# A two-layer decoder in which both feed-forward blocks go from fp32r pairs to pairs of 16-bit floats under powers of two found on the chip, and the token factor goes into the tokens

## The chip, the cores and the metric

The kernel runs on one core of one Trainium2 chip. The metric is the device time in microseconds of one execution, and lower is better. A core has five engines that run their own instruction queues in order: TensorE (PE: matmuls and their weight loads), VectorE (DVE), ScalarE (ACT), GpSimd (POOL) and SyncE (SP, which here starts all the DMA transfers). They wait for each other by semaphores. SBUF is the working memory and PSUM holds the results of matmuls.

## The reference, cut to what matters

1024 tokens of 1024 features run through two layers. Layer 0 mixes three branches of sparse attention and one with sinks, layer 1 a mixture of dilated window attentions; both are followed by a feed-forward block, and this block is what the change is about.

```
D_MODEL = 1024; SEQ = 1024; DEPTH = 2; FFN_HIDDEN = 2816
def rms_norm(x, g):
    y = x * lax.rsqrt(jnp.mean(x * x, axis=-1, keepdims=True) + NORM_EPS)
    return y * g

for layer in range(DEPTH):
    h = rms_norm(x, attn_norm[layer])
    x = x + mixer(h) @ w_out                     # attention of this layer
    h = rms_norm(x, ffn_norm[layer])
    gate, up = jnp.split(h @ w_gate_up[layer], 2, axis=-1)
    x = x + (jax.nn.silu(gate) * up) @ w_down[layer]
return rms_norm(x, final_norm)
```

All inputs are float32.

## The kernel before, in words

**Products of pairs.** Each float32 operand is split in two fp32r tiles: the high part is a rounded copy (ACT), the low part is what is left (`tensor_sub` on DVE or POOL). `gemm` then makes three matmuls for each 128 rows of the contraction: high weight by high token, high by low, low by high. A matmul has a 128x128 weight and 512 columns of tokens, that is, one of two halves of the sequence (`h` is 0 or 1), and adds into a bank of PSUM (`pD`, three of them).

**Feed-forward.** `ffn_jobs` runs over 22 blocks of 128 hidden features (`fi`), gathered in chunks: blocks 0 and 1, then five chunks of four. For each block there is a gate job and an up job (24 matmuls each), for each chunk `down_jobs` with as many weight tiles as the chunk has blocks. The last chunk of the very last block is done by `last_job`. The tokens `n.hT` are only scaled by the gains; the factor 1/rms of each token (`n.R`, made in `norm_close` by a matmul that spreads it over all partitions) is put in after the matmul, in `gated`: gate times R on DVE, tanh on ACT, a product on DVE, a product with R/2. `upped` multiplies by the up result and splits the hidden tile in a pair. `evac` adds the down result to the residual.

**Weights.** Every weight tile is 128x1024 floats (512 KB). `loads` starts its DMA, `splits` makes the high copy on ACT, `lows` the low part on DVE or POOL, whichever `vg` thinks is free sooner. They run some weights ahead of the job that needs them (`loads=4`, `splits=3` in ORDER). A weight takes three tiles of the S4 arena while it is split and two until its job is done. Each weight is loaded and split twice, once for either half of the sequence.

**Order.** The program is written by a list scheduler in Python (`run`): small tasks yield the engine they need next, and the task that could start soonest by a table of costs (`COST`, `LAT`, `SELF`) is written next. The cost of a matmul is the same for 16-bit and fp32r tiles of 512 columns there. The jobs (`dense`) are in this order: projections of layer 0; then for h = 0 and h = 1 the output projection, the feed-forward block and the projections of layer 1; then for h = 0 and h = 1 the output projection and feed-forward block of layer 1. Attention is woven in between: that of layer 0, h = 1 runs beside the first feed-forward block (layer 0, h = 0), that of layer 1, h = 1 beside the third (layer 1, h = 0), part of layer 1, h = 0 beside the second, nothing beside the last. All instructions are recorded by one helper, so that they all have line 209 in the profile; groups are told apart by tiles: `pD` holds projections, `pT` and `pS` scores and small things, `pO` attention outputs; `S` are the large and half-size SBUF tiles, `SM` tiny ones of 128x8.

Of the kernel before, what the change touches and what calls it, by code (L numbers as in the profile page):

```python
# [10 lines left out]
F32 = mybir.dt.float32  # L11
# [16 lines left out]
NF = FFN // P  # L28
SCALE = 0.125
# [4 lines left out]
MAGIC = float(0x5F3759DF)  # L34
INF = float("inf")
# [108 lines left out]
class W:  # L144


    def __init__(self, load, views=None):
        self.load, self.views = load, views
        self.st = self.h = self.l = None
        self.ok = False  # L150

    def split(self, k):
        c = slice(k * P, (k + 1) * P)
        return self.h.w[:, c], self.l.w[:, c]
# [5 lines left out]
    def drop(self):  # L160
        self.h.drop()
        self.l.drop()

# [19 lines left out]
class Norm:  # L183
    def __init__(self):
        self.hT, self.acc, self.ss, self.n = {}, None, None, 0
        self.r = self.R = self.R2 = self.CR = self.SR = self.CK = self.SK = None
        self.uses, self.pairs = 0, False

# [37 lines left out]
class Kernel:  # L226
# [80 lines left out]
    def est(self, *bufs):  # L307

        t = 0.0
        for b in bufs:  # L310
            i = self.info.get((b.raw if isinstance(b, Buf) else b).tensor.name)
            if i is not None:
                t = max(t, i[0])
        return t
# [98 lines left out]
    def more_constants(self):  # L413
        nc, io = self.nc, self.io
        self.sinks = self.const.tile([P, 8], F32, name="sinks", tag="sinks")
        self.sinks8 = self.const.tile([P, 8], F32, name="sinks8", tag="sinks8")
        yield "s"
        self.dma(self.sinks, io["sinks"][0:1, :].to_broadcast([P, 8]))
        for g, src in zip(self.gains[1:], (io["attn_norm"][1], io["ffn_norm"][0], io["ffn_norm"][1], io["final_norm"])):
            yield "s"  # L420
            self.dma(g, src.rearrange("(k p) -> p k", p=P))
        yield "v"
        nc.vector.tensor_scalar(self.sinks8, self.sinks, 1.0 / SCALE, None, op0=ALU.mult)

# [85 lines left out]
    def splits(self):  # L510
        for i, w in enumerate(self.wreq):
            self.wsp = i

            def cond():
                if w.st is None:
                    return INF
                here = self.ends[self.jobi]
                if i < here:
                    return max(self.est(w.st), self.S4.when(2))
                if i >= max(here + self.o.splits, self.ends[self.jobi + 1]):  # L520
                    return INF
                return max(self.est(w.st), self.S4.when(2, RES))
            yield "a", cond
            w.h, w.l = self.S4.take(), self.S4.take()
            for h, l, s in w.parts():
                self.nc.scalar.copy(h, s)
# [22 lines left out]
    def wready(self, w):  # L549
        return self.est(w.h, w.l) if w.ok else INF  # L550
# [27 lines left out]
    def wcols(self, wt, c0):  # L578

        return W(lambda st: self.dma(st.rearrange("p (k c) -> p k c", c=P),  # L580
                                     wt[:, c0:c0 + P].rearrange("(k p) c -> p k c", p=P)))
# [47 lines left out]
    def norm_close(self, n, kind, half=None):  # L629
# [56 lines left out]
        if kind == "ffn":  # L686
            yield "a", self.S2.when
            n.R2 = self.S2.take()
            nc.scalar.activation(n.R2.t, R.t, AF.Copy, scale=0.5)
            y.drop()  # L690
        n.R = R
        for i, b in enumerate(tabs):
            yield "v"
            nc.vector.tensor_mul(b.t, b.t, R.t)
            setattr(n, tables[i][1], b)

# [399 lines left out]
    def cmp_prep(self, key, pe):  # L1096

        nc = self.nc
        pet = self.const.tile([32, 2, 64], F32, tag="pe" + key, name="pe" + key)
        yield "s"  # L1100
        for hh in range(2):
            self.dma(pet[:, hh, :], pe)
        yield "p", lambda: max(self.pS.when(), self.est(pet)) if self.jobi > 1 else INF
# [5 lines left out]
        ps.drop()  # L1109
        yield "vg", lambda: 0.0 if self.zn.get(key, [0, 0])[1] == 2 else INF  # L1110
# [901 lines left out]
    def gu_jobs(self, wt, fi, n, hid, at):  # L2012
# [3 lines left out]
        def gated(acc):  # L2016
# [12 lines left out]
            state["s"] = s  # L2029

        def upped(acc):
            yield "v", self.of(lambda: state.get("s"))
            s = state["s"]
            nc.vector.tensor_mul(s.t, acc.t, s.t)
            acc.drop()
            yield "a", self.S4.when
            t = self.S4.take()
            nc.scalar.copy(t.x[:, 0], s.t)
            yield "vg"
            self.vg(HT, self.o.slack / 2).tensor_sub(t.x[:, 1], s.t, f(t.x[:, 0]))  # L2040
            s.drop()
            hid[at] = t

        def gate(w):
            acc = yield from self.new_acc()
            yield from self.gemm(acc.t, self.stat(w), n.hT.get, KT)
            self.go(gated(acc), 2)

        def up(w):
            acc = yield from self.new_acc()  # L2050
            yield from self.gemm(acc.t, self.stat(w), n.hT.get, KT)
            if fi == NF - 1:
                for b in n.hT.values():
                    b.drop()
            self.go(upped(acc), 2)
        n.uses += 1
        return [Job(24 * MM, gate, [self.wcols(wt, fi * P)]), Job(24 * MM, up, [self.wcols(wt, FFN + fi * P)])]

    def down_jobs(self, wt, fs, hid, h, turn, final):
# [5 lines left out]
        def evac(d, acc):  # L2065
            x = self.xs[h][d]
            yield "v", lambda: 0.0 if x[1] == turn else INF
            self.nc.vector.tensor_add(x[0].t, acc.t, x[0].t)
            acc.drop()
            x[1] += 1  # L2070
            if final:
                yield from final(d, x[0])

        for c in range(nk):
# [4 lines left out]
            def run(w, c=c):  # L2079
                for dd in range(cw // P):  # L2080
                    d = c * (cw // P) + dd

                    def stat(k, tile=False):
                        o = slice(k * cw + dd * P, k * cw + (dd + 1) * P)
                        return w if tile else (w.h.w[:, o], w.l.w[:, o])
                    acc = yield from self.new_acc()
                    yield from self.gemm(acc.t, stat, hid.get, nk)
                    self.go(evac(d, acc), 2)
                if c == nk - 1:
                    for b in hid.values():  # L2090
                        b.drop()
            jobs.append(Job(24 * MM, run, [W(load)]))
# [124 lines left out]
    def ffn_jobs(self, layer, h, n, final):  # L2217
        wg, wd = self.io["w_gate_up"][layer], self.io["w_down"][layer]
        jobs = []
        chunks = [[0, 1]] + [list(range(c, c + 4)) for c in range(2, NF, 4)]  # L2220
        pend = None
        for ci, fs in enumerate(chunks):
            hid = {}
            for i, fi in enumerate(fs):
                jobs += self.gu_jobs(wg, fi, n, hid, i)
# [4 lines left out]
            else:  # L2230
                pend = self.down_jobs(wd, fs, hid, h, ci, final if fs is chunks[-1] else None)
# [69 lines left out]
    def whole(self):  # L2301
# [15 lines left out]
        self.gains = [self.const.tile([P, KT], F32, name=f"gains{i}", tag=f"gains{i}") for i in range(5)]  # L2317
        self.constants()
# [170 lines left out]
```

## Time and profile before

| | |
|---|---|
| time, median of 3 runs | 2752.99 us (2748.75 to 2753.67) |
| the profiled execution | 2751.49 us, of it 2749.7 from the first to the last instruction (the span) |
| mean granted TensorE clock | 0.979 of full speed |
| DMA traffic | 373.85 MB, mean 136 GB/s |

Busy time of an engine is given as a share of the span or of a stretch. Matmuls overlap in the profile, since their ends are modelled: the time of one in a dense row is read from the distance of starts or from the count in a stretch, not from its mean duration.

### The profile page before, as it was taken

To read this page: it belongs to the slowest core of one execution; us is meant where nothing else is said; L and a number is where in the kernel's file an instruction comes from. 1 tells how busy PE (TensorE), PEld (TensorE's weight loads), DVE (VectorE), ACT (ScalarE), POOL (GpSimd) and SP (SyncE) were. 2 spreads that over 40 slices of the span, in tenths; PEclk is the share of its full clock that TensorE was granted. 3 is DMA by queue.
4 is the path that set the end of the run, shared out by engine and by line. 5 is a ranking of instruction groups with operands and counts; after the bars stand their busy time and mean duration, and the time that the engine had idled before them with its cause. 6 is when DMAs were issued, how large, how long until landed. Compare 5 with 4: busy or idle time off the path is not lost. (4 is left out here: it accounts for less than half of the span.)

```text
span 2749.7 us, 40587 instructions
## 1 busy us (share of the span) xinstructions
PE 2635.3 (96%) x15186; PEld 2167.0 (79%) x15186; DVE 1681.4 (61%) x3328; ACT 1146.3 (42%) x1913; POOL 1179.0 (43%) x723
## 2 busy tenths in 40 slices
PE   8888889999999999999999999899999999999998
PEld 7767777777877888778788888778888888788887
DVE  6898877666666785555445667656566665433334
ACT  6465555444444554333333454333333345322222
POOL 4454544433433566444443546343313225544442
PEclk9999999999999999999999999899999999999999
DMA  8765585222332335834344456844544444433330
GB/s 233 211 165 163 155 240 149 74 81 74 105 104 81 119 125 191 250 104 125 94 120 119 140 167 188 234 124 119 155 125 136 130 133 143 140 96 92 100 99 31
DMA packets 447368, 373.85 MB, mean 136 GB/s; under 512 B 54342, under 2 KB 383942, under 8 KB 447172
## 3 DMA queue, kind: packets, MB, share of 16 engines
q1 hardware_dynamic: 447172, 371.26, 46.8%
q8 instruction: 120, 1.97, 0.3%
q14 instruction: 76, 0.62, 0.1%
HBM read 301.42 MB, written 65.30 MB: 133 GB/s over the span
## 5 line engine op out<-in xcount | busy, mean ns | idle before, releaser
L209 PE MATMUL pD<-S,S 128*128 128x512 f32 (+2 forms) x9648 | 2266.5, 388 | 20.5 <-DVE S L209 12.7
L209 PEld LDWEIGHTS pD<-S,S 128*128 128x128 f32 x9648 | 1738.0, 191 | 378.3 <-DVE S L209 15.9
L209 POOL TENSOR_TENSOR S<-S,S 128x1024 fp32r<-128x1024 f32 (+2 forms) x535 | 1023.0, 1925 | 1147.4 <-ACT S L209 618.1
L209 DVE TENSOR_TENSOR S<-pD,S 128x512 f32<-128x512 f32 (+1 forms) x526 | 355.2, 680 | 533.0 <-PE pD L209 514.1
L209 ACT CAST S<-S 128x1024 fp32r<-128x1024 f32 (+2 forms) x571 | 540.2, 984 | 309.3 <-DVE S L209 202.6
L209 DVE TENSOR_TENSOR S<-S,S 128x1024 fp32r<-128x1024 f32 (+4 forms) x243 | 360.9, 1490 | 89.9 <-ACT S L209 88.0
L209 ACT ACTIVATE S<-pT 128x512 f32<-128x512 f32 (+3 forms) x304 | 171.3, 567 | 505.7 <-DVE pT L209 444.4
L209 DVE TENSOR_TENSOR PH<-S,PH 128x512 f16<-128x512 f32 (+3 forms) x265 | 231.4, 877 | 70.8 <-ACT PH L209 69.7
L209 PE MATMUL pT<-S,S 128*128 128x128 f32 (+11 forms) x1072 | 223.7, 336 | 4.1 <-DMA S<-NM 2.5
L209 ACT ACTIVATE S<-S 128x512 f32<-128x512 f32 (+1 forms) x172 | 103.1, 600 | 278.2 <-DVE S L209 277.2
L209 PEld LDWEIGHTS pT<-S,S 128*128 128x128 f32 (+2 forms) x1072 | 196.0, 224 | 24.1 <-DMA S<-NM 3.2
L209 ACT CAST PH<-S 128x512 f16<-128x512 f32 (+3 forms) x304 | 177.1, 589 | 8.5 <-PE pO L209 2.1
L209 PEld LDWEIGHTS <-PH 128*128 128x128 f16 (+1 forms) x3384 | 117.4, 99 | 54.6 <-issue 36.0
L209 DVE TENSOR_TENSOR pT<-pT,S 128x512 f32<-128x512 f32 (+4 forms) x176 | 91.5, 524 | 87.0 <-PE pT L209 86.4
L209 PE MATMUL pO<-S,PH 128*128 128x65 f16 (+1 forms) x3192 | 131.9, 196 | 10.5 <-DVE PH L209 7.2
L209 PE MATMUL pS<-S,S 128*128 128x512 f32 (+3 forms) x460 | 117.9, 348 | 20.1 <-DVE SM L209 13.5
L209 POOL TENSOR_TENSOR PH<-S,PH 128x512 f16<-128x512 f32 (+2 forms) x39 | 48.7, 1250 | 144.4 <-ACT PH L209 144.2
L209 PEld LDWEIGHTS pS<-S,S 128*128 128x128 f32 (+1 forms) x460 | 82.4, 213 | 35.2 <-DVE SM L209 18.7
L209 DVE TENSOR_TENSOR pT<-pT,tDE 128x128 f32<-128x128 f32 (+2 forms) x176 | 64.7, 373 | 70.2 <-PE pT L209 69.3
L209 DVE CUSTOM_DVE_ANT_0 junk<-pS,S 128x256 bf16<-128x256 f32 (+1 forms) x192 | 85.2, 444 | 23.4 <-PE pS L209 16.6
L209 DVE CUSTOM_DVE_ANT_0 junk<-pS,mW 128x512 bf16<-128x512 f32 (+3 forms) x160 | 84.0, 525 | 14.2 <-PE pS L209 8.7
L209 DVE SCALAR_TENSOR_TENSOR S<-S,S 128x512 f32<-128x512 f32 x88 | 67.5, 767 | 38.8 <-ACT S L209 37.8
(163 smaller groups left out, 1028.7 us busy)
## 6 DMA issues: line engine op xcount, KB each, us to landing
S<-in_w_gate_up SPq DMA_DIRECT2D x176, 512.0 KB
S<-in_w_down SPq DMA_DIRECT2D x88, 512.0 KB
S<-in_w_qkv_o SPq DMA_DIRECT2D x48, 512.0 KB
S<-in_w_in_e SPq DMA_DIRECT2D x22, 512.0 KB
mixd<-S SPq DMA_DIRECT2D x18, 512.0 KB
S<-mixd SPq DMA_DIRECT2D x18, 512.0 KB
xd<-S SPq DMA_DIRECT2D x32, 256.0 KB
S<-dhq SPq DMA_DIRECT2D x64, 128.0 KB
```

What stands on the lines that cost most here:

```text
L209: return fn(*a, **kw)
```

## The change

Blocks 2 to 21 of gate and up (`fi >= WIDE`) and the down products of the four middle chunks (`DOWN16`) multiply pairs of float16 instead of fp32r pairs. High and low part of a weight stand side by side in one tile (`W16`). A weight tile is scaled by a power of two: when a tile is loaded for the first time (h = 0), ACT sums its squares (`splits`), a one-column matmul with a tile of ones sums them over the partitions (`over`), four DVE instructions make the power of two and its inverse from the bits of that sum (`power`), and only then is the high part made (`high`) and the low part, on DVE alone (`lows`). For h = 1 the power is known already (`self.scales`). The hidden features of a chunk get a power of their own in `chunk16`. The tokens of these blocks are made again by `halves`: times the token factor R, then times the gain and its power of two, as a float16 pair `n.x16`; `gated16`, `upped` and `evac` undo the powers. Blocks 0 and 1 and the last chunk's down product stay as they were. The `pe` tables of `cmp_prep` move to an S2 tile, and `more_constants` prepares the scaled gains.

```diff
+WIDE = 2
+DOWN16 = True
+NW16 = 2 * (NF - WIDE) + 16
...
+class W16(W):
+    def cut(self, c):
+        a = self.h.f16(2048)
+        return a[:, c], a[:, 1024 + c.start:1024 + c.stop]
...
+            w.h = self.S4.take()
+            if isinstance(w, W16):
+                if w.scale:
+                    self.high(w)
+                else:
+                    acc = self.SM.take()
+                    self.nc.scalar.activation(w.cut(slice(0, 1024))[0], f(w.st.w), AF.Square, accum_out=acc.t[:, 0:1])
+                    self.go(self.ranged(w, acc), lambda i=i: 1 if i < self.ends[self.jobi] + 1 else 3)
+            else:
+                w.l = self.S4.take()
+                for h, l, s in w.parts():
+                    self.nc.scalar.copy(h, s)
+                w.split_ = True
...
+    def high(self, w):
+        self.nc.scalar.activation(w.cut(slice(0, 1024))[0], f(w.st.w), AF.Copy, scale=w.scale["s"])
+        w.split_ = True
+    def power(self, total, out, inv, top=RAISE):
+        nc, i = self.nc, I32
+        nc.vector.tensor_scalar(inv, total, 1e-30, None, op0=ALU.max)
+        nc.vector.tensor_scalar(out.bitcast(i), inv.bitcast(i), -0.5, top, op0=ALU.mult, op1=ALU.add)
+        nc.vector.tensor_scalar(out.bitcast(i), out.bitcast(i), FIELD, None, op0=ALU.bitwise_and)
+        nc.vector.tensor_scalar(inv.bitcast(i), out.bitcast(i), -1.0, float(0x7F000000), op0=ALU.mult, op1=ALU.add)
+    def over(self, acc, n):
+        yield "p", self.pS.when
+        ps = self.pS.take()
+        self.nc.tensor.matmul(ps.t[:, 0:n], self.ones, acc.t[:, 0:n], start=True, stop=True)
+        acc.drop()
+        yield "v"
+        return ps
+    def ranged(self, w, acc):
+        ps = yield from self.over(acc, 1)
+        k = self.wscn % (2 * NW16)
+        self.wscn += 2
+        out, inv = self.wsc[:, k:k + 1], self.wsc[:, k + 1:k + 2]
+        self.power(ps.t[:, 0:1], out, inv)
+        ps.drop()
+        w.scale.update(s=out, inv=inv)
+        yield "a"
+        self.high(w)
...
     def lows(self):
         for i, w in enumerate(self.wreq):
-            yield "vg", lambda: INF if self.wsp <= i else self.est(w.h)
+            yield "v" if isinstance(w, W16) else "vg", lambda: self.est(w.h) if w.split_ else INF
             urgent = i < self.ends[self.jobi] + 1
+            if isinstance(w, W16):
+                h, l = w.cut(slice(0, 1024))
+                self.nc.vector.scalar_tensor_tensor(l, f(w.st.w), w.scale["s"], h, op0=ALU.mult, op1=ALU.subtract)
+                w.st.drop()
+                w.ok = True
+                continue
...
+            for d in range(KT):
+                self.go(self.halves(n, d), 3)
...
+    def halves(self, n, d):
+        nc = self.nc
+        x, g = self.xs[n.half][d][0], n.g16[:, d:d + 1]
+        yield "vg", self.S2.when
+        t = self.S2.take()
+        self.vg(HT).tensor_mul(t.t, x.t, n.R.t)
+        self.used(n)
...
+        b = n.x16s[d // 2]
+        x = b.f16(2048).rearrange("p (d s c) -> p d s c", d=2, s=2)[:, d % 2]
+        nc.scalar.activation(x[:, 0], t.t, AF.Copy, scale=g)
+        yield "v"
+        nc.vector.scalar_tensor_tensor(x[:, 1], t.t, g, x[:, 0], op0=ALU.mult, op1=ALU.subtract)
+        t.drop()
+        n.x16[d] = View(b, x)
...
+        def gated16(acc, w):
+            yield "v", self.SM.when
+            cb = self.SM.take()
+            nc.vector.scalar_tensor_tensor(cb.t[:, 0:1], w.scale["inv"], 0.5, n.g16[:, KT + 1:KT + 2], op0=ALU.mult,
+                                           op1=ALU.mult)
...
+            nc.scalar.activation(s, acc.t, AF.Tanh, scale=cb.t[:, 0:1])
+            yield "v"
+            nc.vector.scalar_tensor_tensor(s, s, 1.0, acc.t, op0=ALU.add, op1=ALU.mult)
             acc.drop()
+            state["c"], state["s"], state["b"] = cb, s, b
...
+            if half:
+                c = state["c"].t
+                nc.vector.scalar_tensor_tensor(c[:, 1:2], w.scale["inv"], n.g16[:, KT + 1:KT + 2], c[:, 0:1], op0=ALU.mult,
+                                               op1=ALU.mult)
+                nc.vector.scalar_tensor_tensor(s, acc.t, c[:, 1:2], s, op0=ALU.mult, op1=ALU.mult)
+                state["c"].drop()
+            else:
+                nc.vector.tensor_mul(s, acc.t, s)
...
+    def chunk16(self, room, hid, at, s):
+        nc = self.nc
...
+        x = [t.f16(2048).rearrange("p (d s c) -> p d s c", d=2, s=2)[:, d] for t in room["tiles"] for d in range(2)]
+        nc.scalar.activation(x[at][:, 0], s, AF.Square, accum_out=room["acc"].t[:, at:at + 1])
+        room["s"][at] = s
+        if len(room["s"]) < 4:
+            return
+        acc, sb = room["acc"], self.SM.take()
+        ps = yield from self.over(acc, 4)
+        sc, inv = sb.t[:, 0:1], sb.t[:, 1:2]
+        nc.vector.tensor_reduce(out=sb.t[:, 2:3], in_=ps.t[:, 0:4], axis=AX.X, op=ALU.add)
+        ps.drop()
+        self.power(sb.t[:, 2:3], sc, inv)
+        room["scale"] = sb
+        def pair(i):
+            yield "a"
+            nc.scalar.activation(x[i][:, 0], room["s"][i], AF.Copy, scale=sc)
+            yield "v"
+            nc.vector.scalar_tensor_tensor(x[i][:, 1], room["s"][i], sc, x[i][:, 0], op0=ALU.mult, op1=ALU.subtract)
...
+            hid[i] = View(room["tiles"][i // 2], x[i])
+        for i in range(4):
+            self.go(pair(i), 2)
...
+            if room is None:
+                self.nc.vector.tensor_add(x[0].t, acc.t, x[0].t)
+            else:
+                sb = room["scale"]
+                self.nc.vector.tensor_mul(sb.t[:, 3 + d % 2:4 + d % 2], sb.t[:, 1:2], w.scale["inv"])
+                self.nc.vector.scalar_tensor_tensor(x[0].t, acc.t, sb.t[:, 3 + d % 2:4 + d % 2], x[0].t, op0=ALU.mult,
+                                                    op1=ALU.add)
...
+            room = {"raw": {}, "read": 0} if 0 < ci < len(chunks) - 1 and DOWN16 else None
```

What stands where in the programs, at three places (names are tile, number and instance; x2 means twice in a row).

PE in the last block, six matmuls of a gate or up job before. Moving tile first, then the weight: the high weight (S_1599) twice, the low one (S_1600) once, and no instruction of its own for loading the weight:

```order
L209 MATMUL pD_25788<-S_1512_24715,S_1599_25677 128x512 x2
L209 MATMUL pD_25788<-S_1512_24715,S_1600_25678 128x512
L209 MATMUL pD_25788<-S_1516_24753,S_1599_25677 128x512 x2
L209 MATMUL pD_25788<-S_1516_24753,S_1600_25678 128x512
```

The same kind of place of the change (last block, a gate or up job):

```order
L242 LDWEIGHTS S_1432_26897
L242 MATMUL pD_27025<-S_1406_26486,S_1432_26897 128x512
L242 LDWEIGHTS S_1432_26897
L242 MATMUL pD_27025<-S_1406_26486,S_1432_26897 128x512
L242 LDWEIGHTS S_1432_26897
L242 MATMUL pD_27025<-S_1406_26486,S_1432_26897 128x512
L242 LDWEIGHTS S_1436_26937
L242 MATMUL pD_27045<-S_1364_25948,S_1436_26937 128x512
```

Each 16-bit matmul has a weight load of its own in the program, and high and low parts are cuts of one tile (S_1432).

PE in the first block (layer 0, h = 0), down products of the first chunk, before:

```order
L209 MATMUL pD_6502<-S_355_6151,S_362_6254 128x512 x2
L209 MATMUL pD_6502<-S_355_6151,S_363_6255 128x512
L209 MATMUL pD_6502<-S_364_6273,S_362_6254 128x512 x2
L209 MATMUL pD_6502<-S_364_6273,S_363_6255 128x512
L209 MATMUL pD_6513<-S_355_6151,S_362_6254 128x512 x2
L209 MATMUL pD_6513<-S_355_6151,S_363_6255 128x512
```

and of the change:

```order
L242 MATMUL pD_6584<-S_356_6221,S_363_6293 128x512 x2
L242 MATMUL pD_6584<-S_356_6221,S_364_6294 128x512
L242 MATMUL pS_6590<-SM_6582,ones 128x1
L242 MATMUL pD_6584<-S_367_6395,S_363_6293 128x512 x2
L242 MATMUL pD_6584<-S_367_6395,S_364_6294 128x512
L242 MATMUL pD_6596<-S_356_6221,S_363_6293 128x512 x2
L242 MATMUL pD_6596<-S_356_6221,S_364_6294 128x512
```

These down products stay in fp32r; a sum over the partitions (`pS_6590`, one column against the ones) has come between two of them.

DVE beside these down products, where their results are added to the residual, before:

```order
L209 TENSOR_TENSOR S_128_5242<-pD_6485,S_128_5242 128x512
L209 TENSOR_TENSOR PH_6491<-S_172_6489,PH_6490 128x512
L209 TENSOR_TENSOR S_131_5324<-pD_6502,S_131_5324 128x512
L209 TENSOR_TENSOR pT_6518<-pT_6518,tDE 128x2x128
L209 TENSOR_TENSOR S_135_5422<-pD_6513,S_135_5422 128x512
L209 TENSOR_TENSOR S_139_5538<-pD_6531,S_139_5538 128x512
L209 TENSOR_TENSOR PH_6537<-S_173_6535,PH_6536 128x512
```

and of the change:

```order
L242 TENSOR_TENSOR S_129_5216<-pD_6567,S_129_5216 128x512
L242 TENSOR_TENSOR PH_6573<-S_180_6571,PH_6572 128x512
L242 TENSOR_SCALAR wsc<-pS_6590 128x1
L242 TENSOR_SCALAR wsc<-wsc 128x1 x3
L242 TENSOR_TENSOR S_133_5336<-pD_6584,S_133_5336 128x512
L242 TENSOR_TENSOR pT_6604<-pT_6604,tDE 128x2x128
L242 TENSOR_TENSOR S_137_5438<-pD_6596,S_137_5438 128x512
L242 SCALAR_TENSOR_TENSOR S_375_6581<-S_370_6478,wsc,S_375_6581 128x1024
L242 TENSOR_TENSOR PH_6626<-S_181_6624,PH_6625 128x512
L242 TENSOR_TENSOR S_140_5530<-pD_6619,S_140_5530 128x512
```

Between the additions stand now the four instructions of a power of two (`wsc`) and a weight's low part of 1024 columns (`S_375`); no low part stood in these rows before.

## Rows read from the trace of the kernel before

**Rows 1.** The page's first part: busy time of each engine, its share of the span, instructions.

```profile
PE 2635.3 (96%) x15186; PEld 2167.0 (79%) x15186; DVE 1681.4 (61%) x3328; ACT 1146.3 (42%) x1913; POOL 1179.0 (43%) x723
```

**Rows 2.** Busy time by stretch of the span: start and end in us, length, busy us (and records) of PE, its weight loads, DVE, ACT and POOL, then the granted clock, the DMA share and GB/s.

```profile
core 0: us, PE busy (x) PEld busy (x) DVE busy (x) ACT busy (x) POOL busy (x), PEclk, DMA share, GB/s
100.00:400.00 300.00, 256.13 (x1869) 207.44 (x1868) 258.02 (x643) 167.55 (x326) 138.37 (x104) 0.91 0.67 194
...
400.00:500.00 100.00, 94.89 (x622) 77.79 (x621) 80.51 (x178) 52.54 (x95) 46.51 (x29) 0.98 0.40 114
500.00:900.00 400.00, 392.85 (x2523) 314.95 (x2522) 249.92 (x489) 171.67 (x280) 148.27 (x88) 1.00 0.32 89
900.00:1000.00 100.00, 97.83 (x674) 81.24 (x673) 80.34 (x158) 56.82 (x93) 55.89 (x33) 1.00 0.40 128
1900.00:2300.00 400.00, 396.19 (x2301) 334.21 (x2302) 250.07 (x553) 150.15 (x258) 118.89 (x85) 1.00 0.50 137
...
2500.00:2600.00 100.00, 100.00 (x432) 80.89 (x431) 34.08 (x36) 27.57 (x33) 50.13 (x28) 1.00 0.32 95
```

**Rows 3.** The chain that ended last, in order of time: start and length in us, engine, tile, count.

```profile
2375.40 334.78 PE pD L209 x1443
```

**Rows 4.** Groups of PE's instructions with the shapes kept apart: count, then busy us and mean ns of one, then idle time before them.

```profile
L209 PE MATMUL pD<-S,S 128*128 128x512 f32 x8400 | 2087.0, 401 | 10.4 <-DVE S L209 7.4 <-DMA S<-mixd 2.9
```

**Rows 5.** PE's instructions in order of time, beside attention: start, length in us, what, count. Two dense groups of 16-bit matmuls (`pO`) and what follows each.

```profile
500.86 0.91 PE L209 MATMUL pO<-S,PH 128*128 128x65 f16 x24
501.60 0.71 PE L209 MATMUL pT<-S,S 128*128 128x512 f32 x2
...
545.81 0.91 PE L209 MATMUL pO<-S,PH 128*128 128x65 f16 x24
546.55 0.42 PE L209 MATMUL pT<-S,kc 128*64 128x512 f32 x1
```

**Rows 6.** The same view around two plain-fp32 matmuls (`pS<-SM,ones`; x2 is one instruction).

```profile
1605.26 3.01 PE L209 MATMUL pD<-S,S 128*128 128x512 f32 x12
1608.20 0.38 PE L209 MATMUL pS<-SM,ones 1*128 1x2 f32 x2
1608.51 0.73 PE L209 MATMUL pD<-S,S 128*128 128x512 f32 x2
...
1731.44 2.26 PE L209 MATMUL pD<-S,S 128*128 128x512 f32 x9
1733.63 0.38 PE L209 MATMUL pS<-SM,ones 1*128 1x2 f32 x2
1733.94 0.97 PE L209 MATMUL pD<-S,S 128*128 128x512 f32 x3
1734.74 0.27 PE L209 MATMUL pS<-ident,MR 128*4 128x128 f32 x1
```

**Rows 7.** Groups of DVE, POOL and ACT instructions with the shapes kept apart (busy us, mean ns of one).

```profile
L209 DVE TENSOR_TENSOR S<-pD,S 128x512 f32<-128x512 f32 x510 | 348.4, 688 | 521.2 <-PE pD L209 502.4 <-DMA S<-xd 7.5 <-ACT S L209 4.0
L209 DVE TENSOR_TENSOR S<-S,S 128x1024 fp32r<-128x1024 f32 x129 | 210.7, 1639 | 30.0 <-ACT S L209 28.5 <-PE pD L209 0.9 <-issue 0.2
...
L209 DVE TENSOR_TENSOR S<-S,S 128x512 fp32r<-128x512 f32 x76 | 106.3, 1401 | 55.5 <-ACT S L209 55.4
L209 DVE SCALAR_TENSOR_TENSOR S<-S,S 128x512 f32<-128x512 f32 x88 | 67.5, 767 | 38.8 <-ACT S L209 37.8
...
L209 DVE SCALAR_TENSOR_TENSOR S<-S,vsc,S 128x512 f16<-128x512 f32 x33 | 35.1, 1068 | 5.6 <-ACT S L209 5.5
...
L209 POOL TENSOR_TENSOR S<-S,S 128x1024 fp32r<-128x1024 f32 x229 | 569.5, 2495 | 369.1 <-ACT S L209 290.8 <-issue 42.1 <-PE pD L209 14.7
...
L209 ACT CAST S<-S 128x1024 fp32r<-128x1024 f32 x358 | 368.0, 1044 | 96.0 <-POOL S L209 43.6 <-DMA S<-in_w_out_o 13.3 <-DMA S<-in_w_qkv_o 10.7
```

**Rows 8.** DVE's instructions on the tiles `SM` and `S`: count, then minimum, median and maximum ns; the last row is the group of the second in the table of groups, with its mean.

```profile
L209 DVE TENSOR_TENSOR SM<-SM x49: 151/162/2383, 28.8 to 2742.3; 128x4 f32<-128x4 f32 x43, 128x2 f32<-128x2 f32 x6
...
L209 DVE TENSOR_SCALAR SM<-SM x27: 141/168/2032, 28.2 to 2740.9; 128x4 int32<-128x4 int32 x9, 1x1 f32<-1x1 f32 x9, 128x4 f32<-128x4 f32 x2, 3x1 f32<-3x1 f32 x2
...
L209 DVE TENSOR_TENSOR S<-S,S x243: 652/1224/3443, 8.2 to 2702.4; 128x1024 fp32r<-128x1024 f32 x65, 128x512 fp32r<-128x512 f32 x38, 128x512 f32<-128x512 f32 x13, 128x816 fp32r<-128x816 f32 x4
...
L209 DVE TENSOR_SCALAR SM<-SM 128x4 int32<-128x4 int32 (+6 forms) x27 | 9.2, 341 | 0.9
```

**Rows 9.** All engines in order of time where the last block begins.

```profile
2362.07 0.69 DVE L209 TENSOR_TENSOR S<-pD,S 128x512 f32<-128x512 f32 x1 [3.32 <-PE pD L209]
2362.79 0.72 ACT L209 ACTIVATE S<-S,gains 128x512 fp32r<-128x512 f32 x1 [3.37 <-DVE S L209]
...
2363.55 0.75 DVE L209 SCALAR_TENSOR_TENSOR S<-S,gains,S 128x512 fp32r<-128x512 f32 x1 [0.79 <-ACT S L209]
...
2375.49 0.59 ACT L209 COPY S<-pS 128x512 f32<-128x512 f32 x1 [7.47 <-PE pS L209]
```

**Rows 10.** PE in order of time: the matmuls that spread the token factor (`pS<-S,ones`) of the first block (layer 0, h = 0) and of the norm after it, the same of the third block (layer 1, h = 0), and the sums for the norm after that.

```profile
464.62 1.07 PE L209 MATMUL pS<-S,ones 128*128 128x512 f32 x2
...
962.58 1.02 PE L209 MATMUL pS<-S,ones 128*128 128x512 f32 x2
...
1838.53 1.02 PE L209 MATMUL pS<-S,ones 128*128 128x512 f32 x2
...
2317.65 0.95 PE L209 MATMUL pS<-onesr,S 128*128 128x2 f32 x8
```

More of the change, by code (lines that the diff above doesn't have):

```diff
@@ L162, in drop, with __init__, cut @@
         self.l.drop()
+class W16(W):
+    def __init__(self, load, scale):
+        super().__init__(load)
+        self.scale = scale
+    def cut(self, c):
+        a = self.h.f16(2048)
+        return a[:, c], a[:, 1024 + c.start:1024 + c.stop]
+    def drop(self):
+        self.h.drop()
+class View:
+    def __init__(self, buf, x):
+        self.raw, self.x = buf.raw, x
 class Heads:
@@ L423, in more_constants @@
         nc.vector.tensor_scalar(self.sinks8, self.sinks, 1.0 / SCALE, None, op0=ALU.mult)
+        for i in (2, 3):
+            yield "a", self.SM.when
+            acc, g = self.SM.take(), self.gains16[i - 2]
+            nc.scalar.activation(g[:, 0:KT], self.gains[i], AF.Square, accum_out=acc.t[:, 0:1])
+            ps = yield from self.over(acc, 1)
+            self.power(ps.t[:, 0:1], g[:, KT:KT + 1], g[:, KT + 1:KT + 2], RAISE - float(5 << 23))
+            ps.drop()
+            nc.vector.tensor_scalar(g[:, 0:KT], self.gains[i], g[:, KT:KT + 1], None, op0=ALU.mult)
     def mask(self, m, conds):
@@ L2009, in out_jobs, with gu_jobs @@
         return jobs
-    def gu_jobs(self, wt, fi, n, hid, at):
+    def gu_jobs(self, wt, layer, fi, n, hid, at, half, room=None):
         nc = self.nc
@@ new lines, in upped @@
+        def upped(acc, w):
+            yield "v", self.of(lambda: state.get("b"))
+            s, b = state["s"], state["b"]
+            if half:
[4 more added lines that the diff above has]
+                state["c"].drop()
+            else:
+                nc.vector.tensor_mul(s, acc.t, s)
+            acc.drop()
+            if room is not None:
+                yield from self.chunk16(room, hid, at, s)
+                return
@@ L2054, in up @@
+            if fi == (NF - 1 if half else WIDE - 1):
+                for b in (n.x16s if half else n.hT).values():
                     b.drop()
[L2055 to L2059, printed above, removed]
+            self.go(upped(acc, w), 2)
+        n.uses += not half
+        sc = [self.scales.setdefault((layer, z, fi), {}) if half else None for z in range(2)]
@@ L2084, in stat @@
                         o = slice(k * cw + dd * P, k * cw + (dd + 1) * P)
-                        return w if tile else (w.h.w[:, o], w.l.w[:, o])
+                        return w if tile else w.cut(o)
                     acc = yield from self.new_acc()
                     yield from self.gemm(acc.t, stat, hid.get, nk)
-                    self.go(evac(d, acc), 2)
+                    self.go(evac(d, acc, w), 2)
                 if c == nk - 1:
-                    for b in hid.values():
+                    for b in hid.values() if room is None else room["tiles"]:
                         b.drop()
-            jobs.append(Job(24 * MM, run, [W(load)]))
+            wq = W(load) if room is None else W16(load, self.scales.setdefault((layer, 2, fs[0], c), {}))
+            jobs.append(Job(24 * MM, run, [wq]))
         return jobs
@@ L2219, in ffn_jobs @@
         jobs = []
+        n.half, n.g16 = h, self.gains16[layer]
+        n.uses += KT
         chunks = [[0, 1]] + [list(range(c, c + 4)) for c in range(2, NF, 4)]
@@ L2230, in ffn_jobs @@
             else:
-                pend = self.down_jobs(wd, fs, hid, h, ci, final if fs is chunks[-1] else None)
+                pend = self.down_jobs(wd, layer, fs, hid, h, ci, final if fs is chunks[-1] else None, n, room)
         return jobs + pend
```

103 lines of the change are left out of this document (69 added, 34 removed).

## The prediction, made blind

> **What bounds the kernel now.** I began with the page's busy times: TensorE (PE) is busy in 96% of the span, VectorE (DVE) in 61%, ScalarE (ACT) in 42%, GpSimd (POOL) in 43% [rows 1]. The table by stretch shows where PE is not full: from 100 to 400 us it is at 85% with DVE at 86%, while in the feed-forward blocks (500 to 900 and 1900 to 2300 hold most of the first half's block of layer 0 and of layer 1, 2500 to 2600 lies inside the last block) it is at 98 to 100% at a granted clock of 1.00, that is 2.4 GHz [rows 2]. The chain that ended last agrees: its longest piece is 1443 projection matmuls in a row, 334.78 us with no wait [rows 3]. So a cheaper matmul shortens the run, and an extra PE instruction lengthens it. DVE is the second engine to watch: 62% beside attention in those first halves, 34% in the last block [rows 2].
>
> **The matmuls.** 8400 of the pD matmuls have 512 columns [rows 4]. In 2500 to 2600 nothing else runs on PE, 432 in 100 us [rows 2], so one takes 231.5 ns. 512 columns at 2.4 GHz take 213.3 ns; 18.2 ns more are paid with each. No row shows a 16-bit matmul of 512 columns. The nearest are attention's, of at most 65 columns, each with a weight load of its own: 24 start at 500.86 and the next group at 501.60, and 24 more take from 545.81 to 546.55 [rows 5]. That is 0.74 us for 24, 30.8 ns each, of which 65 columns are 27.1: an excess of 3.7 ns, 16-bit weight load included. A 16-bit matmul of 512 columns then takes 217.0 ns and saves 14.5. By the order 5376 change type: in each of the four blocks (two layers, two halves) 20 x 2 x 24 in gate and up and 16 x 8 x 3 in down. 5376 x 14.5 ns = **-78 us**. Bounds: no excess at all gives -98; if the 18.2 ns have nothing to do with the number type, 0. I take the value of the 16-bit row, since it holds the part that differs, the weight load.
>
> The Trainium skill, "TensorE: Matmul & The Clock Gate", section "Back-to-back issue gap", gives N/2.4 + 2.5 ns, 215.7 for 512 columns, without a distinction by type. The trace's 231.5 for fp32r disagrees with it. By the page the saving would be an estimated 85 us, 7 more than mine, and the total 7 us lower.
>
> **The small matmuls.** 130 plain-fp32 matmuls of 1 or 4 columns against the 128x128 ones are new: 112 for weights, all in the first halves (56 per layer), 16 for hidden chunks (4 per block), 2 for gains. The nearest row is a plain-fp32 matmul of two columns, which the profile shows as two records [rows 6]. After the pair at 1608.20 the next projection matmul starts 0.31 us later. Ahead of it twelve matmuls take 2.94 us from 1605.26 where 12 x 0.2315 = 2.78 are due; from 1731.44 nine take 2.19 where 2.08 are due: 0.11 to 0.16 more. After the pair at 1733.63 three matmuls take 0.80 where 0.695 are due: 0.10. Together about 0.49 us; 130 x 0.49 = **+63 us**. Lower end 130 x 0.31 = 40, upper end 130 x 0.57 = 74. They break the stream even when nobody waits for them, so I take the middle of what the rows show.
>
> So PE's own account is -78 + 63 = -15 us, unequally spread. A second half saves 1344 x 14.5 = 19 and pays 4 x 0.49 = 2: -17 each. A first half saves 19 and pays 60 x 0.49 = 29: +10 each.
>
> **DVE and ACT in the first halves.** The low part of a weight was made by DVE or POOL and is now always DVE's, and each new power of two takes four tiny DVE instructions. Per first half: 56 lows of 1024 columns. No row has that form; the nearest (512 columns to f16) takes 1.07 us, the subtraction of 1024 columns that it replaces 1.64 [rows 7]. Bounds 1.3 and 2.1; I take 1.6, that of the same size: 90 us. 60 powers x 4 x 0.17 (the median of such a tiny instruction [rows 8]) = 41. Hidden pairs 16 x 1.07 = 17, token pairs 8 x 1.07 = 9, tiny factors 32 x 0.17 = 5. Each of 20 gates loses a PSUM product of 0.69, has its 0.77 row replaced by one of 0.69 and gains two tiny ones: -9. By the order 19 subtractions of 1024 columns (-31) and 23 of 512 (-32, at 1.40) leave DVE. Net +90 us in a block of 480 to 500, from the first factor row to the next norm's [rows 10]: DVE goes from 62% to 81%; with lows at 1.3 and f16 pairs at 0.75, the time of one that met nothing [rows 9], to 76%, with tiny ones at their mean of 0.34 and lows at 2.1 to 97%.
>
> What does that cost PE? At 80% DVE PE was busy 97.8% (900 to 1000) and 94.9% (400 to 500), against 98.6% as the mean of the two first halves now [rows 2]: 0.8 to 3.7 points more idle, 8 to 36 us over 2 x 480. The lower bound is 0 or less: SBUF-to-SBUF subtractions on DVE run from 0.65 to 3.44 us and even tiny ones reach 2.38 [rows 8] while POOL takes 2.50 for one of 1024 columns [rows 7]; by the order 253 of POOL's 473 operations on 512 or 1024 columns of plain tiles and lows are gone, so fewer of DVE's will collide. I take **+4 us**, between 0 and 8.
>
> ACT gains 56 sums of squares of 1024 columns in each first half at about 1.04 [rows 7], 58 us where it is at 38 to 43% [rows 2]: hidden, since weights are prepared up to three jobs of 5.5 us ahead. A weight's new chain (square, tiny matmul, four DVE steps, scale, subtract) sums to 1.04 + 0.31 + 0.7 + 1.04 + 1.6, about 5 us without queueing; if that cover were gone, each of the 112 weights could stall PE by up to 5 us.
>
> **The tokens.** The third gate now needs the token factor, where every gate matmul could once run ahead of it. In the last block the last output column is done at about 2362, so the third gate starts four jobs of 5.55 us later, about 2384; the copy of the factor starts at 2375.49 and takes 0.6 [rows 9]. The first pair needs 0.69 + 0.72 + 0.75 = 2.2 us, each later one at most 1.44 on DVE: the eighth is there at 2388.4, and its matmuls come at 2384 + 7 x 0.69 = 2389. Just hidden; with attention beside it I give **+2 us** in all, and 46 (4 x 8 x 1.44) if there were no cover. At nothing I cost: the gate's bank, held some 2 us through a tanh and a DVE product, where two other banks give 5 us of cover; the same weight transfers; five store-and-reload pairs of mixed heads that go.
>
> **Sum.** -78 + 63 + 4 + 2 = -9 us. The profiled execution took 2751.5 us (span 2749.7 and 1.8 around it), 1.5 under the median of 2753.0: 2751.5 - 9 = 2742.5, say **2743**.
>
> **Rivals.** (B) *DVE late in the first halves:* a projection waits for a low or for a bank, or PE's fixed order reaches a tiny matmul before its square is summed. For it: 14.6% idle at 86% DVE from 100 to 400 us. Against it: DMA is at 67% there too, and 900 to 1000 shows 2.2% at 80% [rows 2]. At 3.7 points it costs 36 instead of 4: 2775; at the 13 points of that stretch 127: 2866. It decides from 13 us, 1.4 points of extra idle, where the sum passes zero. (C) *The change does not do what it says:* 16-bit matmuls run at 231.5 ns as well. Then -9 + 78 = +69: 2820. The 3.7 ns of the 16-bit stream speak against it. (D) *More than I count:* no excess in 16-bit matmuls (-98) and tiny ones at 0.31 (+40), with 4 + 2 as above: -52, 2700.
>
> **How the numbers follow.** About 0.2% (5.5 us) is what a measurement of this kernel can tell from no change: 2747.5 to 2758.5 around the median. Forecast A 0.50, its own range 2725 to 2758 (16-bit matmuls at 215 to 217 ns, tiny ones at 0.4 to 0.57): of it 0.33 lies under 2747.5 and 0.17 above. D 0.14, B 0.31, C 0.05. Faster 0.47, same 0.17, slower 0.36. The range 2700 to 2800 leaves out C, B's upper third and the edge of D, under 2 in 10.
>
> **What would show it.** In the last block about 460 matmuls in 100 us instead of 432, PE still at 100%; if 432 stay, C. The tiny matmuls as 260 records, with the projection stream resuming some 0.3 us after each pair. DVE near 80% in the first halves with POOL below 25%, and PE idle there at 2% or less; if PE is at 95% or less and its waits name DVE or the tiny matmuls, B. No wait of PE over 1 us before the third gate of the last block. My likeliest mistakes are the 0.49 us, taken from one-row and three-row matmuls inside fp32r streams, and the idle at high DVE load, which the stretches bound only loosely.

## The result, and the profile after

The changed kernel takes **2661.23 us** (median of four runs, 2659.32 to 2662.06) against 2751.72 for the kernel before (2748.75 to 2753.67): a ratio of 0.9671, 95% interval 0.9654 to 0.9688. It is 90 us faster. I had forecast 9 us, 2743, with 2700 as the lower end of the range; the time lies 39 us below that.

The page's busy times, to be held against [rows 1]:

```profile
span 2659.2 us, 42231 instructions
PE 2555.7 (96%) x15446; PEld 1712.2 (64%) x15446; DVE 1882.5 (71%) x4266; ACT 1356.3 (51%) x2303; POOL 728.1 (27%) x513
```

PE is busy 79.6 us less, and its idle time (span less busy) went from 114.4 to 103.5, so most of the gain is in PE's own work. The table by stretch, columns as in [rows 2]; the last two rows lie inside the last block:

```profile
500.00:900.00 400.00, 398.49 (x2764) 230.28 (x2763) 304.87 (x824) 256.17 (x437) 58.05 (x52) 1.00 0.35 94
900.00:1000.00 100.00, 96.79 (x700) 81.70 (x701) 80.02 (x157) 58.66 (x95) 44.85 (x31) 1.00 0.44 141
1900.00:2300.00 400.00, 398.11 (x2386) 261.86 (x2387) 271.64 (x755) 220.25 (x374) 88.50 (x67) 1.00 0.52 141
2400.00:2500.00 100.00, 100.00 (x468) 45.62 (x466) 47.25 (x81) 31.61 (x45) 0.00 (x0) 1.00 0.34 100
2500.00:2600.00 100.00, 100.00 (x467) 45.52 (x465) 53.99 (x89) 32.39 (x42) 1.59 (x1) 1.00 0.26 79
```

In the last block PE issues 467 or 468 matmuls in 100 us where it issued 432, at the same granted clock of 1.00. In the first halves (the first and third row) DVE is at 76% and 68%, and PE is nearer to full than before. The four blocks, each from the matmul that spreads its token factor to the next such matmul ([rows 10] show such ends for before), the last one to the end:

```profile
457.91:940.95 483.04, 477.19 (x3334) 290.47 (x3333) 380.18 (x982) 307.14 (x529) 95.73 (x77) 0.99 0.34 95
1152.55:1543.20 390.65, 386.73 (x2172) 215.15 (x2171) 259.19 (x512) 169.57 (x271) 57.82 (x45) 1.00 0.43 122
1773.13:2298.31 525.18, 516.41 (x3071) 339.19 (x3070) 370.16 (x1004) 290.64 (x495) 114.86 (x87) 0.99 0.51 138
2298.31:2659.20 360.89, 344.37 (x1682) 178.29 (x1680) 188.71 (x314) 119.20 (x196) 31.28 (x18) 0.99 0.29 88
```

Now the two prices on which the sum rested. PE's instructions in order of time, in the last block, and the weight loads around the tiny matmul:

```profile
2395.76 39.44 PE L242 MATMUL pD<-S,S 128*128 128x512 f16 x182
2435.04 0.28 PE L242 MATMUL pS<-SM,ones 128*128 128x4 f32 x2
2435.18 5.12 PE L242 MATMUL pD<-S,S 128*128 128x512 f16 x23
...
2434.82 0.41 PEld L242 LDWEIGHTS pS<-SM,ones 128*128 128x128 f32 x2
```

182 matmuls from 2395.76 to 2435.04 are 215.8 ns each. The tiny matmul (two records) starts when they are due to end, and the stream goes on 0.14 us later; its weight load began at 2434.82, while the matmul ahead was still running. I had priced it at 0.49 us.

The groups of PE and DVE that the change adds, shapes kept apart (columns as in [rows 7]):

```profile
L242 PE MATMUL pS<-SM,ones 128*128 128x1 f32 x228 | 33.3, 215 | 3.2 <-ACT S L242 2.4 <-DVE S L242 0.4 <-ACT NM L242 0.3
L242 PE MATMUL pS<-SM,ones 128*128 128x4 f32 x32 | 4.7, 217 | 0.0
...
L242 DVE SCALAR_TENSOR_TENSOR S<-S,wsc,S 128x1024 f16<-128x1024 f32 x224 | 298.8, 1334 | 63.1 <-ACT S L242 62.3
L242 DVE TENSOR_SCALAR wsc<-wsc 128x1 int32<-128x1 int32 x336 | 51.6, 154 | 11.6
```

The 260 records of the 130 tiny matmuls are there. Behind 112 of the 130 a 16-bit product follows, and it starts 0.14 us after the tiny one (median). PE waited 3.2 us in all for their operands (the idle time at the end of the first row): finding a power makes almost nothing late.

### The profile page after: what moved, and what is told of

Same layout as the page of the kernel before. It is cut to its first block, busy times and chain, and to the rows that moved or that the text cites. A ratio compares the mean times of both kernels' runs of the same rounds, so it can differ in the third digit from the quotient of the medians.

```text
span 2659.2 us, 42231 instructions
## 1 busy us (share of the span) xinstructions
PE 2555.7 (96%) x15446; PEld 1712.2 (64%) x15446; DVE 1882.5 (71%) x4266; ACT 1356.3 (51%) x2303; POOL 728.1 (27%) x513
## 5 line engine op out<-in xcount | busy, mean ns | idle before, releaser
L242 PE MATMUL pD<-S,S 128*128 128x512 f16 (+3 forms) x9648 | 2177.5, 378 | 22.6 <-DVE S L242 15.9
L242 PEld LDWEIGHTS <-S 128*128 128x128 f16 x5376 | 509.3, 100 | 586.0 <-issue 42.3
L242 PEld LDWEIGHTS pD<-S,S 128*128 128x128 f32 x4272 | 729.3, 191 | 140.7 <-DVE S L242 5.8
L242 POOL TENSOR_TENSOR S<-S,S 128x512 f32<-128x512 f32 (+3 forms) x279 | 516.4, 1864 | 839.7 <-ACT S L242 716.4
L242 ACT CAST S<-S 128x512 fp32r<-128x512 f32 (+2 forms) x283 | 274.1, 1020 | 154.9 <-DVE S L242 59.7
L242 DVE SCALAR_TENSOR_TENSOR S<-S,wsc,S 128x1024 f16<-128x1024 f32 x224 | 298.8, 1334 | 63.1 <-ACT S L242 62.3
L242 ACT ACTIVATE S<-S 128x1024 f16<-128x1024 f32 (+3 forms) x269 | 210.8, 784 | 142.5 <-DVE S L242 137.8
L242 ACT ACTIVATE S<-S,wsc 128x1024 f16<-128x1024 f32 x224 | 253.7, 1142 | 53.8 <-DVE wsc L242 48.5
L242 DVE TENSOR_TENSOR S<-S,S 128x512 fp32r<-128x512 f32 (+4 forms) x163 | 221.7, 1370 | 57.3 <-ACT S L242 55.1
L242 DVE TENSOR_TENSOR S<-pD,S 128x512 f32<-128x512 f32 (+1 forms) x238 | 156.5, 666 | 109.0 <-PE pD L242 90.8
L242 PE MATMUL pO<-S,PH 128*128 128x65 f16 (+1 forms) x3192 | 131.0, 195 | 10.6 <-DVE PH L242 8.8
```

The lines of the kernel that those rows point to most:

```text
L242: return fn(*a, **kw)
```

## The experiments

Differences from the changed kernel are taken from the two ratios to the kernel before, times 2751.7, since each was run beside the kernel before at another time; "+-" is what the two 95% intervals leave. Stages are named by block: first (layer 0, first half) to fourth (layer 1, second half).

**What a tiny matmul costs.** The same line ahead of each gate and up product, in both kernels; no engine's order changes otherwise, since the scheduler does not count the new line.

```diff
 acc = yield from self.new_acc()
+self.nc.tensor.real.matmul(acc.t[:, 0:1], self.ones, self.ones[:, 0:1], start=True, stop=True)
 yield from self.gemm(acc.t, self.stat(w), ...)
```

> The kernel before, with one more plain-fp32 matmul of one column (ones against a column of ones, into the bank that the next product overwrites) ahead of each of the 176 gate and up products; every engine's order is otherwise that of the kernel before. My prediction's price (0.49 us in a stream of fp32r matmuls) gives 176 x 0.49 = +86: 2838. If such a matmul costs what it shows in the 16-bit streams of the changed kernel, 0.14 us, it gives +25: 2777.

> The same 176 tiny matmuls in the changed kernel, 160 of them ahead of products of 16-bit pairs. Theory S (the price of a tiny matmul was mis-sized: 0.14 us in a 16-bit stream): 160 x 0.14 + 16 x 0.14 to 0.49 = +25 to +30: 2686 to 2691. Rival P (the price of 0.49 holds everywhere and the missing 80 us came from elsewhere): +86: 2747.

Before: 2788.15, ratio 1.0136 (1.0113 to 1.0159): +37 us, **0.21 us** each. After: 2683.53, ratio 0.9761 (0.9746 to 0.9777): +25 +-6, **0.14 us** each. Neither stream pays 0.49; theory S holds and P falls. The expectation of the first, that my price was right at least among fp32r matmuls, is wrong too. Its trace in the last block:

```profile
2455.34 0.28 PE L2052 MATMUL pD<-ones 128*128 128x1 f32 x2
2455.48 5.81 PE L209 MATMUL pD<-S,S 128*128 128x512 f32 x24
2461.13 0.28 PE L2046 MATMUL pD<-ones 128*128 128x1 f32 x2
...
2455.11 0.43 PEld L2052 LDWEIGHTS pD<-ones 128*128 128x128 f32 x2
2455.45 5.40 PEld L209 LDWEIGHTS pD<-S,S 128*128 128x128 f32 x24
```

0.14 us for the tiny one, and 24 fp32r matmuls in 5.65 us where 24 x 0.2315 = 5.56 are due, so 0.09 more behind the break: 0.23 in this place, 0.21 on the average of all 176.

So why did [rows 6] show 0.31 and more? Those matmuls are marked 1*128: their weights stand on one row, the new ones' on 128. The next two runs put that form into the same places.

```diff
-self.nc.tensor.real.matmul(acc.t[:, 0:1], self.ones, self.ones[:, 0:1], start=True, stop=True)
+self.nc.tensor.real.matmul(acc.t[:, 0:2], self.ones[0:1, :], self.ones[0:1, 0:2], start=True, stop=True)
```

> The kernel before with 176 more tiny matmuls as in tiny_in_before, in the same places, but of the form from whose rows I took the price: weights on one row instead of 128 rows (ones on one row by 128 columns, against two columns). Theory K (my 0.49 us belongs to that form, whose weight load begins only when the matmul ahead has left, and not to tiny plain-fp32 matmuls as such): 176 x 0.42 to 0.49 = +74 to +86: 2825 to 2837. Theory Q (it belonged to the places among projections and attention where the rows stood): as in tiny_in_before, +37: 2788.

> The same 176 one-row matmuls in the changed kernel. Theory K: the load of one row stands in the open in a 16-bit stream too, 0.31 us or more each: +55 to +86: 2716 to 2747. Theory Q: as in tiny_in_after, +22: 2684.

Before: 2823.34, ratio 1.0271 (1.0246 to 1.0295): +75 us, **0.42 us** each. After: 2724.31, ratio 0.9908 (0.9882 to 0.9935): +65 +-9, **0.37 us** each. Theory K: the price belongs to the form. (The form also has a second column, but that is not it: the four-column matmul at 2435.04 above costs 0.14.) The trace of the first, in the last block:

```profile
2469.85 2.99 PEld L209 LDWEIGHTS pD<-S,S 128*128 128x128 f32 x13
2473.20 0.29 PEld L2052 LDWEIGHTS pD<-ones 1*128 1x128 f32 x2 [0.36 <-issue]
2473.51 5.40 PEld L209 LDWEIGHTS pD<-S,S 128*128 128x128 f32 x24
...
2473.21 0.38 PE L2052 MATMUL pD<-ones 1*128 1x2 f32 x2
2473.51 5.84 PE L209 MATMUL pD<-S,S 128*128 128x512 f32 x24
2479.28 0.38 PE L2046 MATMUL pD<-ones 1*128 1x2 f32 x2
```

The weight loader stands idle for 0.36 us and begins the one-row load at 2473.20, together with its matmul, where the 128-row load above began 0.23 us ahead of its own. The load lies in the open, and the stream resumes 0.30 us later instead of 0.14. From one tiny matmul to the next it is 6.07 us here and 5.79 above, where the 24 products need 5.56.

The Trainium skill, "TensorE: Matmul & The Clock Gate", section "LDWEIGHTS (loading the stationary operand)", says that a load takes as long for few rows as for 128. The durations agree: one record of the loads in the two runs just shown takes 183 ns on average from one row and 189 from 128, columns as in [rows 7]:

```profile
L2052 PEld LDWEIGHTS pD<-ones 1*128 1x128 f32 x6 | 0.9, 183 | 1.1 <-issue 1.1
...
L2052 PEld LDWEIGHTS pD<-ones 128*128 128x128 f32 x8 | 1.5, 189 | 0.3
```

The cost does not follow from the durations. The same page of the Trainium skill, section "The mechanism", has a load go ahead of running matmuls if it takes other groups of rows or a background weight buffer; a sentence below it allows the overlap "only when row_grp differs". These traces disagree with that sentence: the 128-row load takes the same rows as the matmul ahead and overlaps it. Why the one-row load does not is shown by no run here.

**How much of the gain needs the 16-bit pairs.** First no pair at all, then pairs in gate and up alone.

```diff
-WIDE = 2
-DOWN16 = True
+WIDE = NF
+DOWN16 = False
...
-            for d in range(KT):
-                self.go(self.halves(n, d), 3)
```

> The changed kernel with no 16-bit weights, tokens or hidden values at all (every feed-forward product from fp32r pairs as before); what stays of the change are the gains' preparation, the tables' place and the freed buffers. Theory S: the 16-bit matmuls and what hangs on them give all but some 7 us (the stretch before the first block), so 2745 to 2752. Rival P: much of the gain does not come from the number type, so 2700 or less.

> The changed kernel with 16-bit pairs in gate and up alone, the down product from fp32r pairs throughout. It gives back 1536 of the 5376 cheaper matmuls (1536 x 15.6 ns = 24 us) and saves 48 tiny matmuls. Theory S (0.14 us each): 2661 + 24 - 7 = 2678. Rival P (0.49 us each): 2661 + 24 - 24 = 2661.

Without pairs 2743.33, ratio 0.9972 (0.9961 to 0.9982): 83 of the 90 us need the pairs. Its four blocks last 497.5, 424.6, 535.5 and 375.2 us, each at most 2.0 less than before's. So the rest of the change gives some 8 us; of the 5.9 between the two profiled executions 2.9 lie in the blocks and 3.0 outside. With pairs in gate and up alone (`DOWN16 = False`) 2687.10, ratio 0.9774 (0.9755 to 0.9792): +28 +-7 over the changed kernel, where S gave +17 and P 0. P falls again; S is 11 short, outside the interval too. In its first block PE idles for 13.2 us where it idles for 5.9 in the changed kernel, 7.6 of them waits of attention's 16-bit matmuls for DVE (3.3 in the changed kernel). That is a part of the 11, and in neither theory; the rest stays open.

**What finding the powers costs.** The weights' powers are constants, once with the scheduler free to use the room and once with every order kept (the instruction is still booked in the scheduler and then left out, `mute`).

```diff
-sc = [self.scales.setdefault((layer, z, fi), {}) if half else None for z in range(2)]
+sc = [{"s": self.fixw[:, 0:1], "inv": self.fixw[:, 1:2]} if half else None for z in range(2)]
...
             k.account(key, name, a, kw)
+            if mute:
+                return
```

> The changed kernel with the weights' powers of two written as constants (2048 for gate and up, 4096 for down, which is what these inputs give) instead of found: 112 squares of 1024 columns on ACT, 112 tiny matmuls and 448 tiny DVE instructions go. Theory S (0.13 to 0.14 us for a tiny matmul, the rest hidden): 112 x 0.14 = 16 less: 2645. Rival P (0.49 us each): 55 less: 2606. Rival L (finding the powers makes weights late as well, which a stretch with DVE at 77% could do): well under 2645, with PE's idle time in the first halves falling from 6 and 9 us to about 0.

> As known_powers, but the scheduler still counts the instructions that are left out, so that every engine's order is that of the changed kernel without them (112 squares on ACT, 112 tiny matmuls, 448 tiny DVE instructions less). Theory S: the tiny matmuls alone, 112 x 0.14 to 0.16 = 16 to 18 less than the changed kernel: 2643 to 2645, and the 17 us of idle time that known_powers got came from its other order. If finding the powers costs nothing on the path: 2661. Rival P: 2606.

With a free order 2665.00, ratio 0.9694 (0.9677 to 0.9712): nothing gained, +6 +-7. With the same order 2644.11, ratio 0.9620 (0.9589 to 0.9650): -14 +-10, and 17 by the medians; theory S gave 16 to 18. The two do the same work and stand 21 us apart. Their waits in the third block, us in total, times, longest; first with the free order, then with the kept one:

```profile
PE pT L242 <- ACT S L242: 11.1, 4, 7.4
PE pS L242 <- DVE SM L242: 3.5, 2, 1.8
PE pS L242 <- DVE MR L242: 3.0, 3, 1.9
```

```profile
PE pD L247 <- DVE S L247: 6.0, 2, 5.5
PE pS L247 <- DVE MR L247: 1.2, 2, 0.7
```

In the free order an attention matmul stands in PE's queue ahead of its operand from ACT, and everything behind it waits. That block lasts 533.5 us against 513.2, with 20.0 us idle against 7.5 and a granted clock of 0.96 against 0.99. Rival L, that the finding makes weights late, falls: with the order kept, PE's idle time in the first block is 8.2 us against 5.9 with the finding.

**The waits for the scaled tokens.** PE's waits (as above) in the changed kernel where the second, third and fourth block begin:

```profile
PE pD L242 <- DVE S L242: 3.5, 1, 3.5
...
PE pD L242 <- DVE S L242: 4.5, 2, 4.0
...
PE pD L242 <- DVE S L242: 4.4, 3, 2.6
```

Together 12.4 us, where I had 2. DVE and POOL in the fourth block, in order of time:

```profile
2304.10 2.45 DVE L242 SCALAR_TENSOR_TENSOR S<-S,gains,S 128x512 f16<-128x512 f32 x2
2308.17 4.59 DVE L242 SCALAR_TENSOR_TENSOR S<-S,gains,S 128x512 f16<-128x512 f32 x2
2319.86 0.74 DVE L242 SCALAR_TENSOR_TENSOR S<-S,gains,S 128x512 f16<-128x512 f32 x1
...
2304.32 7.90 POOL L242 TENSOR_TENSOR S<-S,S 128x512 f32<-128x512 f32 x4 [1.29 <-DVE S L242]
```

While POOL forms the tokens' products (2304.32 to 2312.2), a token pair takes DVE 1.2 to 2.3 us; later, with POOL idle, it takes 0.74, close to the 0.75 that I had for all eight. That POOL is the reason is likely but not tested. PE's waits there come right before the third gate and inside it:

```profile
2315.32 1.47 PE L242 MATMUL pD<-S,S 128*128 128x512 f16 x6 [1.34 <-DVE S L242]
2319.39 0.81 PE L242 MATMUL pD<-S,S 128*128 128x512 f16 x3 [2.60 <-DVE S L242]
```

Four kernels try to get these us back. `WIDE = 3`, in both layers or one, and `WIDE = 4` also need hidden chunks that mix both kinds (not printed here); the last edit, the tokens first, is one number.

```diff
-WIDE = 2
+WIDE = 3
...
-            self.go(self.halves(n, d), 3)
+            self.go(self.halves(n, d), 0)
```

> The changed kernel with WIDE = 3: the third gate and up of each block also take fp32r pairs, so the first product that needs the scaled tokens comes 11 us later. 192 matmuls lose 15.6 ns each, +3 us. Theory W (the waits for the scaled tokens, 3.5, 4.5 and 4.4 us in three of the blocks, are what my sum missed on the other side): they vanish, -12 + 3: 2652. If the wait is for DVE's load and only moves: 2664.

> The changed kernel with the scaled tokens' tasks ahead of everything else in the scheduler's ties (priority 0 instead of 3), no work added or removed. Theory W, if the tokens lose time in queues on DVE, POOL and ACT: some 5 of the 12 us come back, 2656. If the chain of eight pairs is itself too long for the cover: 2661, as before.

> WIDE = 4: another 192 matmuls lose 15.6 ns each. Theory W says nothing is left to hide after the third, so 3 us more than with WIDE = 3: 2655.

> WIDE = 3 in layer 1 alone. With WIDE = 3 in both layers the two blocks of layer 1 took 6.8 and 0.9 us less than in the changed kernel, and the stretches ahead of the first and second block, which hold no 16-bit weights, 8.3 and 8.5 us more. If those come with the order of layer 0 and are not paid here: 2661 - 7.7 = 2653. If they come back anyway: 2659 to 2661.

`WIDE = 3`: 2658.81, ratio 0.9666 (0.9649 to 0.9683), the same as the changed kernel. The four blocks last 479.5, 393.1, 518.4 and 360.0 us, together 8.8 less, as theory W has it (-12 + 3); but the stretches ahead of the first and second block last 8.3 and 8.5 us longer (in a profiled execution of 2665.22 us, 6.4 above the median). `WIDE = 4`: 2673.89 in a single run, 19 above W's 2655. Tokens first: 2675.90, ratio 0.9726 (0.9710 to 0.9741), +15 +-6: the one wait at the fourth block's third gate grew to 8.1 us. `WIDE = 3` in layer 1 alone: 2660.56, ratio 0.9673 (0.9646 to 0.9699), where 2653 was hoped for; its profiled execution, 2653.22 us, has 521.7 and 358.7 us in the two blocks, but the other three runs took 2660 to 2663. The waits can be removed where they stand (third block: 8.8 us idle become 3.1 and 4.0); no version turned that into a measurable gain.

## Why the prediction was wrong, point by point

**What bounds it.** Right: PE is at 99, 99, 98 and 95% in the four blocks (the last one includes the kernel's end), and a cheaper matmul shortens the run.

**The matmuls.** Right in mechanism and nearly in size: 215.8 ns instead of 217.0, so 5376 x 15.7 = -84 instead of -78. Rival C (no faster) is out. [rows 2] keep 231.5 for fp32r. The 215.7 ns of the Trainium skill ("TensorE: Matmul & The Clock Gate", "Back-to-back issue gap") agree with the 16-bit stream, the 131 that the same section gives for a sustained stream do not.

**The small matmuls.** This is the step that failed. I took 0.49 us from [rows 6], a matmul with weights on one row, for one with weights on 128. (The terms listed there, 0.31, 0.11 to 0.16 and 0.10, add up to 0.52 to 0.57; 0.49 is below all of that.) The form and the row differ in one mark, 1*128 against 128*128. The runs give 0.42 us for the row's form and 0.21 for the new one in the stream from which I read, and 0.14 for the new one where most of them stand. 130 x 0.14 = +18 (+-5 by the interval) instead of +63: **45 of the 81 us** between forecast and result. My lower bound of 40 us was no bound, since it came from the same rows, and the 0.3 us after which I expected the stream to resume were 0.14. A row with the right mark stood in [rows 10]: eight fp32r matmuls of two columns with weights on 128 rows in 0.95 us, 0.12 each. Two such records, an estimate of 0.24, would have been nearer.

**DVE and ACT.** Right: the lows took 1.33 us (I took 1.6, bounds 1.3 to 2.1), a tiny instruction 0.154 (0.17); DVE is busy 380.2 of 483.0 us in the first block, 79% (81%), POOL 20% (under 25%), PE idle 1.2% (2% or less); in the third DVE is at 70%, PE idle 1.7%. Rival B did not come, and the +4 us for idle time neither. ACT's added squares were hidden but for some 2 us of the waits at the tiny matmuls.

**The tokens.** Wrong by 10 us on the other side: waits of 12.4 us in three blocks instead of +2, in the last one 1.34 us ahead of the third gate, where I said none would pass 1, and 2.60 inside it. My chain put each pair at the duration of one that met nothing, with POOL at work on the same tokens.

**What is left.** With these sizes the sum is -84 + 18 + 12 = -54, or 2697; 36 us of the gain are not in it. (Of the 81 us between forecast and result 45 are the tiny matmuls, 6 the 16-bit matmuls and 4 the idle time; the tokens take 10 back.) Of PE's busy time -84 + 18 = -66 stand against -79.6, so 14 are open; of its idle time, 12 new against a fall of 11, so some 23 us of other waits went away. The 36 do not lie evenly. With these sizes the four blocks should take 12.7, 17.0, 8.2 and 16.1 us less; they take 14.9, 36.0, 10.6 and 14.5 less, and the stretches outside them together 14.5. So 19 of the 36 lie in the second block. Before (columns as in [rows 2]):

```profile
1177.07:1603.67 426.60, 418.46 (x2197) 340.61 (x2196) 224.73 (x396) 154.38 (x239) 188.14 (x103) 0.99 0.43 121
```

Its idle time fell from 8.1 to 3.9 us although 3.5 of the new waits stand there, and 33 of its 1645 matmuls of 256 and 512 columns into `pD` no longer run in it, which moves work and saves none. Of the older waits two kinds fell, over the whole run (us in total, times, longest; before, then after):

```profile
PE pS L209 <- DVE S L209: 14.1, 9, 5.8
...
PE pD L209 <- DVE S L209: 12.7, 8, 2.9
...
PE pD L242 <- DVE S L242: 15.9, 10, 4.0
...
PE pS L242 <- DVE S L242: 3.9, 5, 2.0
```

The first fell by 10.2. The second rose by 3.2 only, with the 12.4 for the tokens in it, so some 9 of its older waits are gone. The longest of the first kind, 5.8 us, stood between the second and the third block (6.3 without pairs); the changed kernel has 8.2 us idle there instead of 16.6, and a granted clock of 0.98 instead of 0.95, which is part of the 14 too. Some 8 us come without the pairs. For the rest the runs show how far such waits move without any change of work, 21 us between the two kernels with known powers and 15 with the tokens first, but not whether a lighter POOL and DVE or the new order took them away. That stays open.

**The rivals.** D, more than I count (-52, chance 0.14), named the right side and one of the right terms, the tiny matmuls at less; the range should have followed it further down.

## What to carry to other kernels

Price an instruction by a row of the same form, and read the marks of rows and columns before the duration: a matmul with weights on one row and one with weights on 128 differ by a factor of two to three in what they cost a dense stream. Where one small instruction is multiplied by a hundred, bounds from rows of one odd form are no bounds. And an experiment on a statically scheduled kernel should keep every engine's order, since the same work in another order moved this one by 21 us.

## What the runs showed of the hardware

- A weight load on one row did not start before the matmul ahead had left (0.36 us of idle loader); the 128-row load started 0.23 us ahead of its own matmul. Cost in a stream of fp32r matmuls 0.42 against 0.21 us, of 16-bit ones 0.37 against 0.14.
- 512 columns take 215.8 ns from 16-bit pairs and 231.5 from fp32r, and a stream of fp32r matmuls loses a further 0.09 us behind a tiny plain-fp32 one.
- DVE's 128x512 f16 pairs took 1.2 to 2.3 us beside POOL's products of the same size and 0.74 with POOL idle, in the one place looked at.
